# Products of zeros among the first transposes and projections, and one weight load moved ahead of another

## The chip, the cores and the metric

The kernel runs on one core of a Trainium2 chip. The metric is the device time of one execution in microseconds; lower is better. The engines are named as in the profile: PE is TensorE (matrix products, its weight loads shown apart as PEld), DVE is VectorE, ACT is ScalarE, POOL is GpSimd and SP is SyncE, which here only issues DMA transfers.

## The reference

One layer of a hybrid decoder on 1024 tokens of width 1024, with 16 meta tokens put in front, all in float32:

```python
u = rmsnorm(h, g_pre_mix[l])
z = u @ w_in[l]
q, k, v, xr, yr = jnp.split(z, split_at, axis=-1)
attn = sliding_window_attention_with_sinks(...)
...                                  # conv(4), gated linear recurrence, GeLU gate
mix = jnp.concatenate([attn.astype(h.dtype), rec], axis=-1) @ w_out[l]
h = h + rmsnorm(mix, g_post_mix[l])
u = rmsnorm(h, g_pre_ffn[l])
f = jnp.square(jax.nn.relu(u @ w_ff1[l])) @ w_ff2[l]
h = h + rmsnorm(f, g_post_ffn[l])
```

`w_in` is 1024 x 1792, `w_ff1` 1024 x 4096 and `w_ff2` 4096 x 1024.

## The kernel before, in words

Every float32 operand is split into a high and a low part, and a product is made of three products: high by high, high by low, low by high. `mm3` issues the three at lines 125, 130 and 131; `part` (line 309) issues one of the three for all eight blocks `kc` of 128 rows, and `project` uses `mm3`. A split is a cast on ACT (line 96) and a subtraction on DVE (line 99).

The token rows are normalised, transposed on PE, 128 columns at a time, and split into `u`, eight pairs of tiles tagged "a". The tokens come in four pieces; the first one, `ALL[0]`, has 272 rows: 16 meta rows `xm` and two blocks `xa` and `xb` of 128 rows each. `transposed_first` handles it. Its inner function `turn` (line 401) chains the transposes in a fixed order: six blocks of `xa`, the gains `g_r`, six blocks of `xm`, six blocks of `xb`. Blocks `kc` 6 and 7 are transposed whole (line 426), once the banks of blocks 0 and 1 have been read. After each block, `split_scaled` scales and casts it on ACT (line 117) and subtracts on DVE (line 118). The first projections of K and V then follow through `part` (line 309): `wk` high by `u` high, `wk` high by `u` low, the same for `wv`, and the third parts.

PE has nothing to do until the first rows are normalised. In that time `load` (line 339) issues products of a tile of zeros into a bank `idle` that nobody reads: 11 of them, each of 512 columns.

A scheduler that estimates times orders the instructions of each engine at build time; `behind` and `chained` add fixed orders where they are wanted. Tiles come from pools by tag ("raw", "ws", "a", "b", "c", "d", "e"), each with a number of buffers, and a new tile waits until the buffer that it gets is free. The PSUM banks come from four tags of two banks each ("acc", "pt", "o", "s").

Behind the attention, the recurrence and the output projection stands the feed-forward part. Its first product is done by blocks with sums of blocks (a Strassen-like scheme): `prep_a(p)` loads two tiles `r0` and `r1` of `w_ff1` (512 KB each, `w1_load`, line 1185), forms sums of their halves on DVE (line 1188) and splits them. Some blocks are wanted before any sum and are loaded alone by `early`: two loads of 256 KB each. The last call, `early(1, 2, pair("a", ESH), "a")`, fills an "a" tile; `loads[0]` holds the name of its last load. `prep_a` puts the load of `r0` behind that load and leaves the load of `r1` free. All of these loads go through SP's queue, in the order in which the scheduler put them.

Of the kernel before, what the change touches and what calls it, by code (L numbers as in the profile page):

```python
# [10 lines left out]
F32R = mybir.dt.float32r  # L11
# [5 lines left out]
P = 128  # L17
# [20 lines left out]
def hybrid_layer(  # L38
# [6 lines left out]
    nc = tc.nc  # L45
# [12 lines left out]
    def slot(tag, shape, dt=F32):  # L58
        uid[0] += 1
        return slab.tile(shape, dt, tag=tag, name=f"{tag}{uid[0]}", bufs=bufs[tag])  # L60
# [242 lines left out]
            sink(acc[:, :n], t0, n)  # L303


    def part(acc, w, piece, k, last=2):
        t0, n = piece
        for kc in range(KC):
            last_mm[0] = nc.tensor.matmul(  # L309
                acc[:, :n], w[k // 2][:, kc, :], u[kc][k % 2][:, t0 : t0 + n],  # L310
                start=k == 0 and kc == 0, stop=k == last and kc == KC - 1,
                skip_group_check=True,
            ).ins.name

    ALL = [(0, 272), (272, 256), (528, 256), (784, 256)]
    REAL2 = [(16, 512), (528, 512)]
# [7 lines left out]
    for h in range(2):  # L324
        nc.gpsimd.memset(f32(kl[h][HALF[1 - h]]), 0.0)

    zeros = slot("ws", [P, 512], F32R)
    nc.vector.memset(f32(zeros), 0.0)
    km = slot("ws", [P, 4, 2 * P], F32R)
    nc.gpsimd.memset(f32(km[:, 0:2, 0 : P - NMETA]), 0.0)  # L330
# [3 lines left out]


    idle = bank("acc")
    def load(n, cols, after=None):
        for _ in range(n):
            ins = nc.tensor.matmul(
                idle[:, :cols], zeros[:, :P], zeros[:, :cols], start=True, stop=True,  # L340
                skip_group_check=True,
            ).ins
            if after:
                behind(after, ins)
        return ins.name

    load(11, 512)

    def normed(b):
        if b == 0:  # L350
# [12 lines left out]
    def chained(e, ins):  # L363
        if last[e] is not None:
            behind(last[e], ins)
        last[e] = ins.name
# [29 lines left out]
    def transposed_first(xn):  # L396
        (xm, _), (xa, _), (xb, _) = xn
        n, order = ALL[0][1], [None]

        def turn(dst, src):  # L400
            ins = nc.tensor.transpose(dst, src, ident[: src.shape[0], : src.shape[0]]).ins
            if order[0]:
                behind(order[0], ins)
            order[0] = ins.name

        def cols(kc):
            return slice(kc * P, (kc + 1) * P)

        pts = []
        for kc in range(6):  # L410
            pts.append(bank(("o", "s", "pt")[kc % 3]))
            turn(pts[kc][:, NMETA : NMETA + P], xa[:, cols(kc)])
        pg = bank("acc")
        turn(pg[:, :8], g_r)
        chained(0, nc.scalar.copy(g_mix_col, pg[:, :8]).ins)
        for kc in range(6):
            turn(pts[kc][:, :NMETA], xm[:NMETA, cols(kc)])
        for kc in range(KC):
            if kc < 6:
                pt = pts[kc]  # L420
                turn(pt[:, NMETA + P : n], xb[:, cols(kc)])
            else:
                pt = bank(("o", "s")[kc - 6])
                o = 0
                for x_, m in xn:
                    nc.tensor.transpose(pt[:, o : o + m], x_[:m, cols(kc)], ident[:m, :m])
                    o += m
            uh, ul = u[kc]
            high = split_scaled(
                uh[:, :n], ul[:, :n], pt[:, :n], g_mix_col[:, kc : kc + 1]  # L430
            )
            chained(0, high[0])
            chained(1, high[1])
            mark[0] = high[1].name

    def fetch(cols, tag="raw", pieces=1):
        raw = slot(tag, [P, KC, P])
# [25 lines left out]
    chained(0, nc.scalar.copy(wk[0][:, 0:4], rk[:, 0:4]).ins)  # L463
    last[1] = scaled[0]
    chained(1, nc.vector.tensor_copy(wk[0][:, 4:8], rk[:, 4:8]).ins)
    transposed_first(xn)
    low_w(wk, rk)
    wv = high_w(rv, "b")
    low_w(wv, rv)
# [89 lines left out]
    for b in range(4):  # L559
        if b:  # L560
            transposed(b, xn if b == 1 else normed(b), done[b])
        piece = ALL[b]
        if b == 0:

            acc = [bank("acc"), bank("acc")]
            for a, w in zip(acc, (wk, wv)):
                part(a, w, piece, 0)
                part(a, w, piece, 1)
            xn = [(norm_rows(xt[2], True), P)]
            xn.append((norm_rows(xt[3], True), P))  # L570
            part(acc[0], wk, piece, 2)
            sink_k(acc[0][:, : piece[1]], *piece)
            part(acc[1], wv, piece, 2)
            sink_v(acc[1][:, : piece[1]], *piece)
            wq1 = high_w(rq1)
            low_w(wq1, rq1)
            for w, (t0, n), sink, tag in (
                (wq, (16, 256), sink_q0, "o"), (wq1, (16, 256), sink_q1, "acc"),
            ):
                acc = bank(tag)  # L580
                for k in range(3):
                    part(acc, w, (t0, n), k)
# [631 lines left out]
    def prep_a(p, late=None):  # L1214
        r0 = slot("raw", [P, 4, 256])
        behind(loads[0], w1_load(r0, 0, p, 0, 2))
        r1 = slot("a" if 2 <= p < 14 else "d", [P, 4, 256])
        w1_load(r1, 1, p, 0, 2)
        a11, a21, a12, a22 = r0[:, :, LO], r0[:, :, HI], r1[:, :, LO], r1[:, :, HI]
        sums = [  # L1220
            combine(a22, a21, a22, ALU.add), combine(a21, a11, a21, ALU.subtract)
# [514 lines left out]
```

## Time and profile before

| | |
|---|---|
| median of 3 runs | 944.97 us (944.78 to 945.34) |
| the profiled execution's own time | 945.26 us |
| its span, first to last instruction | 943.3 us |
| PE busy | 934.0 us (99%) |
| DVE, ACT, POOL busy | 664.7, 505.1, 132.9 us |
| mean granted TensorE clock | 0.999 |
| PE's first product of zeros starts | 1.51 us |
| the first transpose starts | 6.94 us |
| the first projection product starts | 9.57 us |

Times inside a run are microseconds from the first instruction. In a row of the timeline stand the start, the duration, the engine, the line, the operation, the tiles (output <- inputs), the shape, how many instructions were merged into the row, and in brackets how long the engine had been idle and what ended that. The duration of a PE product holds the way through the array too, so products overlap: how fast they follow one another is seen from their starts.

### The profile page before, as it was taken

To read this page: it belongs to the slowest core of one execution; us is meant where nothing else is said; L and a number is where in the kernel's file an instruction comes from. 1 tells how busy PE (TensorE), PEld (TensorE's weight loads), DVE (VectorE), ACT (ScalarE), POOL (GpSimd) and SP (SyncE) were. 2 spreads that over 40 slices of the span, in tenths; PEclk is the share of its full clock that TensorE was granted. 3 is DMA by queue.
4 is the path that set the end of the run, shared out by engine and by line. 5 is a ranking of instruction groups with operands and counts; after the bars stand their busy time and mean duration, and the time that the engine had idled before them with its cause. 6 is when DMAs were issued, how large, how long until landed. Compare 5 with 4: busy or idle time off the path is not lost.

```text
span 943.3 us, 12158 instructions
## 1 busy us (share of the span) xinstructions
PE 934.0 (99%) x4562; PEld 780.8 (83%) x4562; DVE 664.7 (70%) x846; ACT 505.1 (54%) x846; POOL 132.9 (14%) x204
## 2 busy tenths in 40 slices
PE   8999999999999999999999999999999999999997
PEld 7999999877888888888888888888888888888886
DVE  7667788889877986755544465477667676779794
ACT  8546765679434854443655575653533443445441
POOL 4104436430021200110000000001121000001200
PEclk9999999999999999999999999999999999999999
DMA  8220011104359768573422364334777755647934
GB/s 275 58 67 23 24 46 46 46 23 142 101 182 291 234 192 287 180 255 123 157 89 90 116 219 120 103 113 115 198 171 177 210 179 189 191 155 208 242 65 90
DMA packets 99911, 136.49 MB, mean 145 GB/s; under 512 B 24391, under 2 KB 63319, under 8 KB 99853
## 3 DMA queue, kind: packets, MB, share of 16 engines
q1 hardware_dynamic: 90652, 110.67, 36.7%
q0 software_dynamic: 8736, 23.67, 11.8%
q10 hardware_dynamic: 464, 1.38, 0.4%
q8 instruction: 36, 0.59, 0.3%
q14 instruction: 23, 0.18, 0.1%
HBM read 113.60 MB, written 21.50 MB: 143 GB/s over the span
## 4 chain that ended last, share of the span: by engine, by line
PE 98%; DVE 0%; DMA 0%; ACT 0%; issue 0%; DVEq 0%; ACTq 0%
PE ps_acc L125 12%; PE ps_acc L131 11%; PE ps_acc L130 11%; PE ps_pt L130 7%; PE ps_pt L125 7%; PE ps_pt L131 7%; PE ps_s L125 6%; PE ps_s L131 6%; PE ps_s L130 6%; PE ps_o L125 5%; PE ps_o L130 5%; PE ps_o L131 5%; PE ps_o L763 2%; PE ps_acc L988 1%; PE ps_acc L309 1%; PE ps_s L693 1%
## 5 line engine op out<-in xcount | busy, mean ns | idle before, releaser
L99 DVE TENSOR_TENSOR ws<-raw,ws 128x1024 fp32r<-128x1024 f32 (+1 forms) x69 | 83.6, 1212 | 74.3 <-ACT ws L96 23.3
L96 ACT CAST ws<-raw 128x1024 fp32r<-128x1024 f32 (+1 forms) x68 | 69.7, 1026 | 80.8 <-PE ps_o L130 32.6
L96 ACT CAST ws<-e 128x1024 fp32r<-128x1024 f32 x41 | 43.0, 1050 | 84.9 <-PE ps_o L130 37.8
L99 DVE TENSOR_TENSOR b<-b,b 128x1024 fp32r<-128x1024 f32 (+1 forms) x49 | 57.7, 1179 | 27.0 <-PE ps_o L130 21.7
L130 PE MATMUL ps_acc<-a,ws 128*128 128x512 f32 (+3 forms) x224 | 76.3, 341 | 0.0
L125 PE MATMUL ps_acc<-a,ws 128*128 128x512 f32 (+3 forms) x224 | 76.3, 341 | 0.0
L131 PE MATMUL ps_acc<-a,ws 128*128 128x512 f32 (+3 forms) x224 | 75.7, 338 | 0.0
L99 DVE TENSOR_TENSOR ws<-e,ws 128x1024 fp32r<-128x1024 f32 x41 | 50.2, 1224 | 31.2 <-ACT ws L96 17.8
L96 ACT CAST b<-b 128x1024 fp32r<-128x1024 f32 (+1 forms) x49 | 49.5, 1011 | 41.5 <-DVE b L1188 35.3
L750 POOL TENSOR_SCALAR_AFFINE_SELECT c<-c 128x512 fp32r<-128x512 f32 x64 | 51.4, 817 | 75.2 <-ACT c L96 66.1
L131 PE MATMUL ps_acc<-ws,b 128*128 128x512 f32 (+1 forms) x120 | 46.1, 384 | 0.0
L130 PE MATMUL ps_acc<-ws,b 128*128 128x512 f32 (+1 forms) x120 | 46.1, 384 | 0.0
L125 PE MATMUL ps_acc<-ws,b 128*128 128x512 f32 (+1 forms) x120 | 46.0, 385 | 0.0
L125 PEld LDWEIGHTS ps_acc<-a,ws 128*128 128x128 f32 x224 | 42.2, 188 | 3.1 <-DVE b L997 0.3
L131 PEld LDWEIGHTS ps_acc<-a,ws 128*128 128x128 f32 x224 | 42.2, 188 | 3.0
L130 PEld LDWEIGHTS ps_acc<-a,ws 128*128 128x128 f32 x224 | 42.1, 188 | 2.8
L130 PE MATMUL ps_pt<-ws,b 128*128 128x512 f32 x112 | 44.2, 395 | 0.0
L125 PE MATMUL ps_pt<-ws,b 128*128 128x512 f32 x112 | 44.2, 394 | 0.0
L131 PE MATMUL ps_pt<-ws,b 128*128 128x512 f32 x112 | 44.0, 393 | 0.0
L125 PE MATMUL ps_s<-ws,b 128*128 128x512 f32 x110 | 43.4, 395 | 0.0
L130 PE MATMUL ps_s<-ws,b 128*128 128x512 f32 x110 | 43.3, 393 | 0.0
L131 PE MATMUL ps_s<-ws,b 128*128 128x512 f32 x110 | 43.2, 393 | 0.0
(436 smaller groups left out, 2679.8 us busy)
## 6 DMA issues: line engine op xcount, KB each, us to landing
raw<-in_w_ff_dram SPq DMA_DIRECT2D x59, 512.0 KB
e<-in_w_ff_dram SPq DMA_DIRECT2D x43, 512.0 KB
a<-in_w_ff_dram SPq DMA_DIRECT2D x12, 512.0 KB
s_dram<-a POOLq DMA_DIRECT2D x12, 512.0 KB, 3.8
raw<-in_w_in_dram SPq DMA_DIRECT2D x9, 512.0 KB
c<-in_x_dram SPq DMA_DIRECT2D x8, 512.0 KB
d<-in_x_dram SPq DMA_DIRECT2D x8, 512.0 KB
out_dram<-raw SPq DMA_DIRECT2D x8, 512.0 KB
```

Of the source, the lines that this page charges most:

```text
L96: cast[0] = nc.scalar.copy(hi, src).ins.name
L99: low = nc.vector.tensor_tensor(lo, src, f32(hi), op=ALU.subtract).ins
L125: ins = nc.tensor.matmul(dst, lh, rh, start=start, stop=False, skip_group_check=True).ins
L130: nc.tensor.matmul(dst, lh, rl, start=False, stop=False, skip_group_check=True)
L131: last_mm[0] = nc.tensor.matmul(dst, ll, rh, start=False, stop=stop, skip_group_check=True).ins.name
L309: last_mm[0] = nc.tensor.matmul(acc[:, :n], w[k // 2][:, kc, :], u[kc][k % 2][:, t0 : t0 + n], start=k == 0 and kc == 0, stop=k == last an ...
L693: nc.tensor.matmul(dst, q[h][:, c], hi, start=True, stop=False, skip_group_check=True,)
L750: nc.gpsimd.affine_select(out=p_[:, :, s], in_=f32(p_[:, :, 0]), pattern=[[0, 4], [g, P]], compare_op=op, fill=0.0, base=0, channel_multip ...
L763: nc.tensor.matmul(two[:, :, oc : oc + w], v, p_.rearrange("p (j i) s c -> p j (i s c)", j=2)[:, :, pc : pc + w], start=n == 0 and k == 0, ...
L988: ins = nc.tensor.matmul(y2_bank[half], (wh, wh, wl)[k][:, kc, :], (uh, ul, uh)[k][:, t0 : t0 + n], start=m % 24 == 0, stop=m % 24 == 23, ...
```

## The change

It has four parts.

1. `zeros` has 128 columns where it had 512. The products of 512 columns read it four times over, through an operand that repeats the one block.
2. In front of the first transposes stand 13 products of zeros instead of 11.
3. Ten more products of zeros, of 128 columns each, go into a bank `pad` at fixed places: two in front of the transposes of `xb`, two behind them, and behind the first products of `part` two, one, one, none, none, one and one for `kc` 0 to 6 (`PADS`).
4. `prep_a(0)` puts the load of `r1`, too, behind `early`'s last load.

```diff
-    def part(acc, w, piece, k, last=2):
+    def part(acc, w, piece, k, last=2, pads=None):
         t0, n = piece
         for kc in range(KC):
-            last_mm[0] = nc.tensor.matmul(
+            ins = nc.tensor.matmul(
...
+            if pads and kc < len(pads[0]):
+                behind(pads[2], ins)
+                pads[2] = load(pads[0][kc], pads[1], ins.name)
+            last_mm[0] = ins.name
...
-    zeros = slot("ws", [P, 512], F32R)
+    zeros = slot("ws", [P, P], F32R)
...
-    def load(n, cols, after=None):
+
+    def load(n, dst, after=None):
+        cols = dst.shape[-1]
+        rhs = zeros
+        if cols > P:
+            dst = dst.rearrange("p (a b) -> p a b", b=P)
+            rhs = zeros.rearrange("p (a b) -> p a b", a=1).to_broadcast([P, cols // P, P])
         for _ in range(n):
             ins = nc.tensor.matmul(
-                idle[:, :cols], zeros[:, :P], zeros[:, :cols], start=True, stop=True,
-                skip_group_check=True,
+                dst, zeros, rhs, start=True, stop=True, skip_group_check=True
             ).ins
...
-    load(11, 512)
+    load(13, idle)
...
+        pad = bank("acc")
         for kc in range(6):
             turn(pts[kc][:, :NMETA], xm[:NMETA, cols(kc)])
+        order[0] = load(2, pad[:, :P], order[0])
         for kc in range(KC):
+            if kc == 6:
+                order[0] = load(2, pad[:, :P], order[0])
...
+        return [PADS, pad[:, :P], order[0]]
+
+    PADS = (2, 1, 1, 0, 0, 1, 1)
...
-                part(a, w, piece, 0)
+                part(a, w, piece, 0, pads=pads)
+                pads = None
...
-        w1_load(r1, 1, p, 0, 2)
+        ins = w1_load(r1, 1, p, 0, 2)
+        if p == 0:
+            behind(loads[0], ins)
```

The instruction streams differ at these places and nowhere else, apart from which semaphore a few instructions wait on. The first place is on PE, from the last transpose of `xb` to the first projection products. `ps_acc_262` (later `ps_acc_269`) is the bank of the K projection, `ps_o_223` and `ps_s_229` (`ps_o_230`, `ps_s_236`) are the banks of blocks 6 and 7. Before:

```order
L401 MATMUL ps_pt_194<-ident,d_147 128x128
L309 MATMUL ps_acc_262<-a_89,b_180 128x272
L309 MATMUL ps_acc_262<-a_91,b_180 128x272
L426 MATMUL ps_o_223<-ident,d_128 128x16
L426 MATMUL ps_o_223<-ident,d_135 128x128
L426 MATMUL ps_o_223<-ident,d_147 128x128
L309 MATMUL ps_acc_262<-a_93,b_180 128x272
L426 MATMUL ps_s_229<-ident,d_128 128x16
L426 MATMUL ps_s_229<-ident,d_135 128x128
L426 MATMUL ps_s_229<-ident,d_147 128x128
```

In the changed kernel, at the same place on PE, where line 349 is the product of zeros and `ps_acc_201` the bank `pad` (lines 309, 411 and 440 are 309, 401 and 426 of before):

```order
L411 MATMUL ps_pt_196<-ident,d_149 128x128
L349 MATMUL ps_acc_201<-ws_111 128x128 x2
L309 MATMUL ps_acc_269<-a_89,b_182 128x272
L349 MATMUL ps_acc_201<-ws_111 128x128 x2
L309 MATMUL ps_acc_269<-a_91,b_182 128x272
L349 MATMUL ps_acc_201<-ws_111 128x128
L440 MATMUL ps_o_230<-ident,d_130 128x16
L440 MATMUL ps_o_230<-ident,d_137 128x128
L440 MATMUL ps_o_230<-ident,d_149 128x128
L309 MATMUL ps_acc_269<-a_93,b_182 128x272
L349 MATMUL ps_acc_201<-ws_111 128x128
L440 MATMUL ps_s_236<-ident,d_130 128x16
```

The transposes and projection products keep their order; a product of zeros now stands ahead of each group of whole transposes, too.

The second place is in SP's queue, around the start of the feed-forward part. `d_3559` (later `d_3572`) is `r1` of `prep_a(0)`, `a_3494` (`a_3507`) is the "a" tile of `early`'s last call, `raw_3557` (`raw_3570`) is `r0` of `prep_a(0)`. Before, with the semaphores that each load waits for:

```order
L1129 DMA out_dram<-raw_3333 128x1024 [waits DVE_49]
L1185 DMA d_3559<-in_w_ff_dram 128x4x256 [waits PE_49]
L1185 DMA a_3494<-in_w_ff_dram 128x4x128 [waits DMAHW7_49]
L1185 DMA a_3494<-in_w_ff_dram 128x4x128 [waits DMAHW0_49]
L1185 DMA raw_3557<-in_w_ff_dram 128x4x256 [waits DMAHW5_49,DMAHW1_49,Activation_49]
```

In the changed kernel, in the same place of SP's queue:

```order
L1147 DMA out_dram<-raw_3346 128x1024 [waits DVE_49]
L1203 DMA a_3507<-in_w_ff_dram 128x4x128 [waits PE_49]
L1203 DMA a_3507<-in_w_ff_dram 128x4x128 [waits DMAHW7_49]
L1203 DMA d_3572<-in_w_ff_dram 128x4x256 [waits DMAHW0_49,PE_49]
L1203 DMA raw_3570<-in_w_ff_dram 128x4x256 [waits DMAHW5_49,DMAHW1_49,Activation_49]
```

The 512 KB load of `r1` went behind the two loads of 256 KB; the load of `r0` stays fourth.

More of the change, by code (lines that the diff above doesn't have):

```diff
@@ L312, in part @@
                 skip_group_check=True,
-            ).ins.name
+            ).ins
+            if pads and kc < len(pads[0]):
+                behind(pads[2], ins)
+                pads[2] = load(pads[0][kc], pads[1], ins.name)
+            last_mm[0] = ins.name
     ALL = [(0, 272), (272, 256), (528, 256), (784, 256)]
@@ L344, in load @@
                 behind(after, ins)
-        return ins.name
-    load(11, 512)
+            after = ins.name
+        return after
+    load(13, idle)
     def normed(b):
@@ L465, in hybrid_layer @@
     chained(1, nc.vector.tensor_copy(wk[0][:, 4:8], rk[:, 4:8]).ins)
-    transposed_first(xn)
+    pads = transposed_first(xn)
     low_w(wk, rk)
```

## Prediction

> **What bounds the kernel now.** I read the page first: the span, the busy shares, the granted clock and the chain of waits by engine.
>
> ```profile
> span 943.3 us, 12158 instructions
> PE 934.0 (99%) x4562; PEld 780.8 (83%) x4562; DVE 664.7 (70%) x846; ACT 505.1 (54%) x846; POOL 132.9 (14%) x204
> PEclk9999999999999999999999999999999999999999
> PE 98%; DVE 0%; DMA 0%; ACT 0%; issue 0%; DVEq 0%; ACTq 0%
> ```
>
> PE is busy for 99% of the span, at full granted clock in every slice, and it is 98% of the chain that ended last. A change can save time only where PE waits or where its own products become fewer or faster. So the second view is the list of waits of PE over the whole span, and the third is busy time by windows (columns: the window, its length, then busy us and instruction count of PE, PEld, DVE, ACT and POOL, the granted clock, the DMA share, GB/s).
>
> ```profile
> PE ps_acc L339 <- DVE base_e L627: 1.5, 1, 1.5
> PE ps_o L401 <- DVE d L248: 1.0, 2, 0.8
> ```
>
> ```profile
> 6.20:9.50 3.30, 2.34 (x19) 1.85 (x19) 2.94 (x8) 2.38 (x7) 0.20 (x1) 1.00 1.19 325
> 9.50:12.20 2.70, 2.63 (x13) 1.78 (x13) 2.65 (x7) 2.70 (x9) 0.00 (x0) 1.00 1.12 326
> 12.20:300.00 287.80, 287.74 (x1712) 254.91 (x1712) 230.39 (x353) 176.42 (x412) 85.65 (x134) 1.00 0.30 91
> 300.00:350.00 50.00, 50.00 (x230) 40.67 (x229) 41.70 (x66) 37.21 (x71) 6.77 (x11) 1.00 0.72 224
> 350.00:930.00 580.00, 580.00 (x2537) 472.30 (x2536) 377.84 (x396) 280.56 (x337) 34.72 (x40) 1.00 0.55 162
> ```
>
> The two waits both lie in the first 9 us. From 12.20 to 930 PE is busy for 917.74 of 917.80 us. Two things follow. The load that moves in SP's queue, near 314, has no PE wait to remove. And whatever the first 12 us lose or gain reaches the end in full, because nothing behind them has slack.
>
> The fourth view is the timeline of those 12 us.
>
> ```profile
> 0.98 0.48 DVE L328 MEMSET ws<- 128x512 f32 x1 [0.98 <-PEq L1720]
> 1.41 0.06 DVE L627 MEMSET base_e<- 128x4 f32 x1
> 1.51 4.66 PE L339 MATMUL ps_acc<-ws 128*128 128x512 f32 x11 [1.51 <-DVE base_e L627]
> 6.94 0.30 PE L401 MATMUL ps_o<-ident,d 128*128 128x128 f32 x1 [0.77 <-DVE d L248]
> 7.07 0.27 PE L401 MATMUL ps_s<-ident,d 128*128 128x128 f32 x1
> 7.18 0.27 PE L401 MATMUL ps_pt<-ident,d 128*128 128x128 f32 x1
> ...
> 8.16 0.21 PE L401 MATMUL ps_s<-ident,d 16*128 16x16 f32 x1
> 8.22 0.21 PE L401 MATMUL ps_pt<-ident,d 16*128 16x16 f32 x1
> 8.63 0.30 PE L401 MATMUL ps_o<-ident,d 128*128 128x128 f32 x1 [0.20 <-DVE d L248]
> 9.03 0.49 ACT L117 ACTIVATE a<-ps_o,gcol 128x272 fp32r<-128x272 f32 x1 [0.89 <-PE ps_o L401]
> 9.20 0.27 PE L401 MATMUL ps_pt<-ident,d 128*128 128x128 f32 x1
> 9.55 0.50 DVE L118 SCALAR_TENSOR_TENSOR a<-ps_o,gcol,a 128x272 fp32r<-128x272 f32 x1 [0.34 <-ACT a L117]
> 9.56 0.19 PEld L309 LDWEIGHTS ps_acc<-a,b 128*128 128x128 f32 x1 [0.33 <-ACT a L117]
> 9.94 0.19 PEld L309 LDWEIGHTS ps_acc<-a,b 128*128 128x128 f32 x1 [0.19 <-ACT a L117]
> 10.27 0.60 PE L426 MATMUL ps_o<-ident,d 16*128 16x16 f32 x3
> 10.62 0.37 PE L309 MATMUL ps_acc<-a,b 128*128 128x272 f32 x1
> 10.93 0.60 PE L426 MATMUL ps_s<-ident,d 16*128 16x16 f32 x3
> 11.26 0.52 ACT L117 ACTIVATE a<-ps_o,gcol 128x272 fp32r<-128x272 f32 x1
> 11.28 5.31 PE L309 MATMUL ps_acc<-a,b 128*128 128x272 f32 x37
> 11.63 0.53 ACT L117 ACTIVATE a<-ps_s,gcol 128x272 fp32r<-128x272 f32 x1
> 12.21 4.17 PEld L309 LDWEIGHTS ps_acc<-a,b 128*128 128x128 f32 x33 [0.19 <-ACT a L117]
> ```
>
> PE sits behind others here. The first transpose waits for DVE's normalised rows (0.77 us idle), the transposes of `xb` wait for DVE again (0.20), and the first eight projection products follow ACT, which casts one block after another: 9.03 for the first, 11.26 and 11.63 for the last two, so one each 0.37 us. The last of them lets PE go at 12.21, and from there PE streams.
>
> **The change part by part.** The profiled execution took 945.26 us, its span 943.3 and 1.96 around it; it lies 0.29 above the median of the runs, 944.97. The sum below is made against the execution and then moved to the median.
>
> *Smaller tile of zeros.* Filling 512 columns took 0.48 us and 4 columns 0.06, so 128 columns are estimated, on the line between, at 0.16. The products of zeros start 0.32 earlier, at 1.19. DVE idles behind the fill until its rows arrive, so nothing else moves. Worth nothing by itself.
>
> *Two more products in front.* The speed of such a product changes on the way:
>
> ```profile
> L339 PE MATMUL ps_acc<-ws x11: 397/628/796, 1.5 to 5.8; 128*128 128x512 f32 x11
> 317.70 0.39 PE L125 MATMUL ps_s<-b,b 128*128 128x512 f32 x1
> 317.93 0.39 PE L130 MATMUL ps_s<-b,b 128*128 128x512 f32 x1
> ```
>
> The eleven start between 1.5 and 5.8, so they follow each other by 0.43 at the median duration of 628 ns; a product of this size later follows by 0.23 (317.70 to 317.93). The shortest, 397 ns, has the duration of those later ones, so the speed doubled near the end of the eleven; I put it at 5.5, some 4.0 us behind the first. The granted-clock column does not show the slow start; the durations do. Two more cost 0.46 to 0.86. The eleven ended at 6.17, so the thirteen end between 6.17 - 0.32 + 0.46 = 6.31 and 6.71. The first transpose waits for DVE until 6.94, which covers them. If all thirteen ran slowly, they would end at 1.19 + 0.80 + 12 x 0.43 = 7.15, 0.21 late. I take 0, bounds 0 and +0.21.
>
> *Ten small products.* No row has a product of this type with 128 columns. The nearest are the transposes of 128 columns, which follow each other by 0.11 (7.07 to 7.18); I take 0.11 for each. [...]
>
> I stay with the row, for each of the ten:
>
> - Two ahead of the transposes of `xb`: small transposes follow each other by 0.06 (8.16 to 8.22), so PE is free near 8.28, and 0.22 more end at 8.50. DVE lets the next go at 8.63. Hidden; at twice the price 0.09 late.
> - Two behind those: 9.20 + 0.11 + 0.22 = 9.53, and ACT lets the first projection product go at 9.56. Hidden, by little, but a delay here does not reach ACT, whose input is ready.
> - Two behind the first projection product: a product of 272 columns takes 0.14 at most (5.31 for 37), so 9.56 + 0.14 + 0.22 = 9.92, before the next at 9.94. Hidden.
> - One behind the second: 9.94 + 0.14 + 0.11 = 10.19. The transposes of block 6 start at 10.27, since their bank is read by DVE until 9.55 + 0.50 = 10.05. Hidden, or up to 0.11 late if the time from 10.05 to 10.27 is PE's own.
> - One behind the third, at 10.62. The transposes of block 7 followed at 10.93 with no wait that the profile shows, and ended at 10.93 + 0.60 = 11.53. Between the end of a first transpose (8.63 + 0.30 = 8.93) and ACT's cast (9.03) lie 0.10, and 11.53 + 0.10 is 11.63: ACT's last cast has no slack. This product costs 0.11, through ACT and the last projection product, to the end; 0 if it fits into the 0.17 between 10.62 + 0.14 and 10.93.
> - The two behind the sixth and seventh run while PE waits for ACT (0.19 idle ahead of 12.21). Hidden.
>
> Sum: +0.11; lower bound 0, since nothing that sets 6.94, 8.63 or ACT's pace gets faster; upper bound with the thirteen late as well, 0.21 + 0.09 + 0.11 + 0.11 = +0.52.
>
> *The load moved in SP's queue.* Today `r1` ("d") is issued first, then the two halves of the "a" tile.
>
> ```profile
> 313.64 0.43 SPq L1185 DMA_DIRECT2D d<-in_w_ff_dram  x1
> 314.12 1.58 SPq L1185 DMA_DIRECT2D a<-in_w_ff_dram  x2
> 320.11 1.05 ACT L96 CAST a<-a 128x1024 fp32r<-128x1024 f32 x1 [0.63 <-DMA a<-in_w_ff_dram]
> 322.39 0.69 DVE L1188 TENSOR_TENSOR d<-raw,d 128x512 f32<-128x512 f32 x1
> 330.56 0.39 PE L125 MATMUL ps_pt<-b,a 128*128 128x512 f32 x1
> ```
>
> Afterwards the "a" halves go first. The 1 MB of the three lands by 320.11, whatever its order. `r1` then comes last, at about 320.1, and DVE wants it at 322.39: 2.3 us of slack. The "a" tile is cast up to 0.63 earlier, but PE takes it only at 330.56. The new wait of the "a" load on PE cannot hold the queue: before, it stood behind `r1`, whose own wait on PE covered it. I take 0; below nothing is excluded because PE has no wait there, and above nothing takes more than 2.3 us of delay.
>
> So the profiled execution would become 945.26 + 0.11 = 945.37, and the median 944.97 + 0.11 = 945.08.
>
> **The rivals.**
>
> *The clock falls back today, and the small products prevent it (faster).* Between the end of the zeros at 6.17 and the first projection product at 9.57, PE has 3.4 us with only transposes and waits. If PE then lost its speed and took 4.0 us to regain it, as at the start, it would run slowly until 13.6. From 12.21 that is 1.4 us at half speed, 0.7 lost. A median that holds such executions would fall to 944.97 - 0.7 = 944.3. For it speaks how long the stretch is. Against it: in this execution the clock column is 1.00 in both windows, the products from 11.28 on take 0.14 each, and three runs lie within 0.56 us. [...]
>
> *The repeated operand runs slower (slower).* No row shows a product that reads one block four times. The thirteen have 6.94 - 1.19 = 5.75 us, 0.44 each; from there on they delay the first transpose. Were each the price of four transposes, 0.44 fast and 0.88 slow, about 4.6 would run in the 4.0 slow us and 8.4 x 0.44 = 3.7 follow: they end at 8.9, 1.95 late. The slack ahead of 8.63 (8.28 to 8.63) takes back 0.35, so 1.6 stay: 946.6. If the speed never doubled, 13 x 0.88 ends at 12.6, 5.7 late and 5.3 net: 950.3. Against it: four pieces of one operand are still 512 columns in one instruction.
>
> *`r1` lands late (slower).* Behind two other loads it could come later than 322.39; DVE is busy 41.70 of 50 us in that window and would push its splits back, and PE would wait for the excess over 2.3 us. It would take a landing of 4.2 us later than I expect to be seen: 946.9.
>
> *The change does nothing*: all products hide, 944.97. That is my lower bound; it lies in the forecast.
>
> **How the numbers follow.** The measurement can tell about 0.2%, 1.9 us, from no change. The forecast, 0 to +0.5, has 0.80; the clock rival 0.10, of which 0.03 for more than one fall and so over 1.9 us; the repeated operand 0.06, of which 0.05 over 1.9 us; the late `r1` 0.02, half of it visible; other causes 0.02, half to each side. Faster: 0.03 + 0.01 = 0.04. Slower: 0.05 + 0.01 + 0.01 = 0.07. Within: 0.89. The runs scatter from 944.78 to 945.34; with 0 to +0.5 that is 944.78 to 945.86. Downwards the range takes in the clock rival at 944.3, with 0.1 below it, and upwards 0.14 for another scatter of the runs: 944.2 to 946.0.
>
> **What would show it right or wrong.** Right: the products of zeros end before 6.94; the first transpose, 8.63 and 9.03 stay; block 7's transposes and ACT's last cast come about 0.1 later; the last projection weight load stands near 12.3; PE still shows no wait from there to 930; the "a" cast near 319.5 and `r1`'s sum still at 322.4. Wrong: a first transpose behind 6.94 that waits for PE itself (repeated operand); products of 272 columns at 0.23 or more (clock); a wait of PE between 322 and 345 (`r1`); or a shift at 12.21 that does not reappear at the end.

## The result, and the profile after

The changed kernel takes 946.86 us (median of 20 runs, 945.12 to 947.57), the kernel before took 945.08 in the same comparison (20 runs, 944.71 to 946.62): a ratio of 1.0014, with an interval of 1.0008 to 1.0020. The prediction was 945.1, with a range of 944.2 to 946.0. (The ratio of the two medians is 1.0019, that of the means 1.0014.) Single runs scatter by over 2 us, with 16 of the changed kernel's 20 and 2 of before's 20 above 946, so a profile need not be typical: the changed kernel's took 945.68 (span 943.6) and is one of its shortest runs, the one of before took 945.26.

The first 12 us of the changed kernel, in the timeline:

```profile
0.90 0.17 DVE L332 MEMSET ws<- 128x128 f32 x1 [0.90 <-PEq L1740]
1.12 4.81 PE L349 MATMUL ps_acc<-ws 128*128 128x512 f32 x13 [1.12 <-DVE base_e L645]
6.96 0.30 PE L411 MATMUL ps_o<-ident,d 128*128 128x128 f32 x1 [1.03 <-DVE d L248]
8.66 0.30 PE L411 MATMUL ps_o<-ident,d 128*128 128x128 f32 x1
9.06 0.49 ACT L117 ACTIVATE a<-ps_o,gcol 128x272 fp32r<-128x272 f32 x1 [0.89 <-PE ps_o L411]
9.83 0.33 PE L349 MATMUL ps_acc<-ws 128*128 128x128 f32 x2
10.20 0.22 PE L349 MATMUL ps_acc<-ws 128*128 128x128 f32 x1
11.08 0.60 PE L440 MATMUL ps_s<-ident,d 16*128 16x16 f32 x3
11.71 0.49 ACT L117 ACTIVATE a<-ps_s,gcol 128x272 fp32r<-128x272 f32 x1
12.25 0.42 PEld L309 LDWEIGHTS ps_acc<-a,b 128*128 128x128 f32 x3
```

The thirteen products end at 1.12 + 4.81 = 5.93 and PE then waits 1.03 for DVE, as before. Block 7's transposes come at 11.08 for 10.93, ACT's last cast at 11.71 for 11.63, the last wait for ACT ends at 12.25 for 12.21. That is the +0.1 of the sum, at 0.04 to 0.08.

The rest of the loss lies over 300 us further on. SP's queue, the sum of `prep_a(0)` on DVE, and the products of PE near 333, from the timelines of the changed kernel:

```profile
313.60 1.32 SPq L1203 DMA_DIRECT2D a<-in_w_ff_dram  x2
315.02 0.64 SPq L1203 DMA_DIRECT2D d<-in_w_ff_dram  x1
317.95 0.37 SPq L1203 DMA_DIRECT2D raw<-in_w_ff_dram  x1
319.34 1.05 ACT L96 CAST a<-a 128x1024 fp32r<-128x1024 f32 x1
323.87 0.69 DVE L1206 TENSOR_TENSOR d<-raw,d 128x512 f32<-128x512 f32 x1 [1.44 <-DMA raw<-in_w_ff_dram]
324.48 0.75 DVE L1161 TENSOR_SCALAR d<-raw,rs 128x1024 f32<-128x1024 f32 x1
333.14 1.69 ACT L96 CAST b<-a 128x256 fp32r<-128x256 f32 x3 [0.22 <-DVE a L1206]
333.17 0.40 PE L131 MATMUL ps_pt<-b,a 128*128 128x512 f32 x1
333.58 0.76 DVE L99 TENSOR_TENSOR b<-a,b 128x256 fp32r<-128x256 f32 x2
333.60 0.50 PE L125 MATMUL ps_acc<-b,e 128*128 128x512 f32 x1
334.06 0.50 PE L130 MATMUL ps_acc<-b,e 128*128 128x512 f32 x1
334.40 0.39 PE L131 MATMUL ps_acc<-b,e 128*128 128x512 f32 x1
```

The same places in the kernel before:

```profile
323.84 0.75 DVE L1143 TENSOR_SCALAR d<-raw,rs 128x1024 f32<-128x1024 f32 x1 [0.77 <-POOL rs L172]
332.52 1.70 ACT L96 CAST b<-a 128x256 fp32r<-128x256 f32 x3 [0.22 <-DVE a L1188]
332.95 0.77 DVE L99 TENSOR_TENSOR b<-a,b 128x256 fp32r<-128x256 f32 x2
333.13 0.39 PE L131 MATMUL ps_pt<-b,a 128*128 128x512 f32 x1
333.36 0.40 PE L125 MATMUL ps_acc<-b,e 128*128 128x512 f32 x1
333.59 0.40 PE L130 MATMUL ps_acc<-b,e 128*128 128x512 f32 x1
```

DVE's sum started at 322.39 before and starts at 323.87 now, behind a wait of 1.44 us for the `raw` tile, which is `r0`. The scale behind it comes at 324.48 for 323.84, 0.64 later. The last splits of `t_sums`, whose results PE reads as `b`, come as much later nine microseconds on: ACT's casts at 333.14 for 332.52, DVE's lows at 333.58 for 332.95. Nothing is made up on the way. In before, PE took the first cast at 333.36, 0.84 behind its start; here it takes it at 333.60, 0.46 behind, so before had 0.38 us in hand, and 0.62 less 0.38 is lost at once: the product comes 0.24 later. (The products ahead of it ran 0.04 later, at 333.17 for 333.13.) Then PE meets the later casts and lows. Its products follow by 0.43, 0.46 and 0.34 us, where 0.23 each is their pace in before (333.13, 333.36, 333.59): 0.54 us lost. The busy time of PE in the window 300:350 (columns as in the prediction) hides most of that, since a waiting product is shown longer (the one at 333.60 as 0.50, for 0.40 at 333.36 in before):

```profile
300.00:350.00 50.00, 49.97 (x227) 40.20 (x226) 41.10 (x65) 36.84 (x70) 6.37 (x11) 1.00 0.72 221
```

PE does 227 products in it where it did 230.

### The profile page after: what moved, and what is told of

Read it like the earlier page. It is cut to its first block, busy times and chain, and to the rows that moved or that the text cites. A ratio compares the mean times of both kernels' runs of the same rounds, so it can differ in the third digit from the quotient of the medians.

```text
span 943.6 us, 12181 instructions
## 1 busy us (share of the span) xinstructions
PE 935.0 (99%) x4574; PEld 781.9 (83%) x4574; DVE 664.5 (70%) x846; ACT 505.2 (54%) x846; POOL 134.4 (14%) x204
## 4 chain that ended last, share of the span: by engine, by line
PE 99%; DMA 0%; DVE 0%; ACT 0%; DVEq 0%; issue 0%
PE ps_acc L125 12%; PE ps_acc L130 11%; PE ps_acc L131 11%; PE ps_pt L130 7%; PE ps_pt L125 7%; PE ps_pt L131 7%; PE ps_s L125 6%; PE ps_s L131 6%; PE ps_s L130 6%; PE ps_o L125 5%; PE ps_o L130 5%; PE ps_o L131 5%; PE ps_o L781 2%; PE ps_acc L1006 1%; PE ps_acc L309 1%; PE ps_s L711 1%
```

## The experiments

Theory S: the whole loss is the moved load; `r0` lands later, DVE waits for it, and PE for DVE. The rivals are named with each run. In each comparison the kernel before ran on the same chip. It had medians of 945.19, 945.04, 944.87 and 945.06 in the four, and lay above 946 in 19 of its 128 runs, those of the result included.

**The change once more.** No edit.

> The changed kernel once more, for a second profile of it. Theory A (SP's queue): r1 stands behind the two halves of the a tile, the loads around it land late, the sums of prep_a(0) wait on DVE and PE waits near 333; the excess over before in the median (1.8 us) is that wait, so this profile shows PE gaps between 333 and 345 of 0.5 to 2.5 us in total, as much as its own time is above 945.1. Theory B (zeros): the excess comes from the first 14 us, the last projection weight load of the first eight stands between 12.3 and 14, and the gaps near 333 stay at 0.6 or less whatever the time.

Measured 947.02 (946.12 to 947.43, 11 runs, all above 946), ratio 1.0016 [1.0007, 1.0025]. The profiled run, 946.57, is longer than the first one, and shows the same place with a larger wait:

```profile
324.72 0.69 DVE L1206 TENSOR_TENSOR d<-raw,d 128x512 f32<-128x512 f32 x1 [1.65 <-DMA raw<-in_w_ff_dram]
334.45 0.49 PE L125 MATMUL ps_acc<-b,e 128*128 128x512 f32 x1 [0.69 <-ACT b L96]
```

**The load alone.** The kernel before, with part 4.

```diff
-        w1_load(r1, 1, p, 0, 2)
+        ins = w1_load(r1, 1, p, 0, 2)
+        if p == 0:
+            behind(loads[0], ins)
```

> The kernel before with part 4 alone: the load of r1 of prep_a(0) behind early's last load, no change to the products of zeros. Theory A: +1.3 to +1.9 us over before, DVE's first sum of prep_a(0) waits for its loads by 1 to 4 us and PE has gaps near 333. Theory B: within 0.3 us of before.

Measured 947.03 (945.16 to 947.57, 9 of 11 runs above 946), ratio 1.0013 [1.0004, 1.0021]. DVE waits 2.61 us, PE 1.23, and PE's busy time in the window 330:350 is that much short:

```profile
325.07 0.69 DVE L1188 TENSOR_TENSOR d<-raw,d 128x512 f32<-128x512 f32 x1 [2.61 <-DMA raw<-in_w_ff_dram]
334.80 0.50 PE L125 MATMUL ps_acc<-b,e 128*128 128x512 f32 x1 [1.23 <-ACT b L96]
330.00:350.00 20.00, 18.77 (x80) 14.47 (x79) 16.80 (x31) 12.90 (x21) 1.73 (x3) 1.00 0.61 196
```

**The zeros alone, and the front alone.** The changed kernel without part 4, and the kernel before with parts 1 and 2.

```diff
# zeros alone
-        ins = w1_load(r1, 1, p, 0, 2)
-        if p == 0:
-            behind(loads[0], ins)
+        w1_load(r1, 1, p, 0, 2)
# front alone: parts 1 and 2, no small products
-    load(11, 512)
+    load(13, idle)
```

> The changed kernel without part 4: the small tile of zeros, 13 products in front and the ten small ones, and SP's queue as before. Theory A: +0.05 to +0.3 us over before (the 0.11 of the prediction), no PE gap near 333. Theory B: +1.3 to +1.9 us.

> The kernel before with parts 1 and 2 alone: the tile of zeros of 128 columns and 13 products in front, none of the ten small ones. Theory A: within 0.2 us of before. Theory B, if the repeated operand or the clock is at fault: more than +1 us; if the ten small products are at fault: within 0.2 us of before while the run without part 4 shows the excess.

Measured 945.02 (3 of 11 runs above 946), ratio 0.9999 [0.9990, 1.0008], and 945.18 (1 of 11), ratio 0.9997 [0.9988, 1.0006]. The products of zeros are worth nothing that can be measured; the loss is part 4. The profile of the zeros alone happens to be one of its three long runs, 946.68, with the same signature, a sum at 324.93 behind `r0`. Its load order is that of before, so the weak place is there without part 4, and is met less often.

Half of the long runs of before, and the longest of them, have another mark, though. For 108 of its runs, those of the four comparisons, the mean granted clock is on record. 17 of them lie above 946 us, and 9 of these 17 have a clock of 0.994 to 0.997, where most of its runs have 0.998 or 0.999. Of the nine above 946.5, eight have the lower clock. Over all kernels, `shift` (below) left aside, 19 of 171 runs without the ten small products have it, and none of 99 runs with them. No run of before with the lower clock was kept as a trace, so where the clock fell in it is not shown.

**When `r0` lands.** The traces of before and of the changed kernel hold 16 semaphore events for `r0`, from 321.25 to 321.71 and from 321.10 to 323.75; they are counted here as portions of the load that have landed. From these events, in us, with the order in SP's queue:

```
kernel       order in the queue   r0 issued   14 of 16   last     sum starts
before       r1, a, a, r0         317.99      321.61     321.71   322.39
front alone  r1, a, a, r0         318.22      321.91     322.12   322.62
zeros alone  r1, a, a, r0         318.59      322.71     324.85   324.93
after        a, a, r1, r0         317.95      321.86     323.75   323.87
after again  a, a, r1, r0         318.06      322.96     324.60   324.72
load alone   a, a, r1, r0         317.94      322.15     324.95   325.07
```

The bulk of `r0`, 14 portions, lands by 321.6 to 323.0 whatever the order; one or two portions come later, the last of them 1.6 to 2.8 us behind it, in the three traces with `r1` right ahead of `r0` and in the long run of the zeros. DVE waits for the last portion: the sum starts 0.12 us behind it in the three traces of part 4, at 323.87 for 323.75, 324.72 for 324.60 and 325.07 for 324.95.

**More time for DVE.** The sums that read `r0` behind the last combine of `t_sums(8:12)`, in the changed kernel and in the kernel before.

```diff
-    t_sums(slice(8, 12))
-    wa[0] = prep_a(0)
+    summed_8 = t_sums(slice(8, 12))
+    wa[0] = prep_a(0, summed_8)
```

> The changed kernel, with prep_a(0)'s two sums put behind the last combine of t_sums(8:12), so that DVE does four sums, a scale and one low, some 3 us of work, before it first needs r0. Theory S (the whole loss is DVE waiting at its sum for r0's last portions, and the lows of ot2 coming late to PE behind that): no idle time of PE near 333, even if r0 still lands at 323.5 to 325, and a median of 945.0 +- 0.4, with few runs above 946. Theory P (part 4 costs PE something by itself, by its waits or its traffic, wherever DVE stands): still about 946.9, most runs above 946. If the reordering itself costs (r1, r0's splits come later to the first products that read them), PE waits at another place, between 334 and 345, and the time is above 946 with that gap in the trace.

> The kernel before, with the same reordering on DVE and nothing else. Theory S: before has the same exposure, with its r0 landing at 321.7 for a want at 322.39, so that about one run in five is at 947; with the reordering these go, the median is 944.9 to 945.1 and no more than one run in ten lies above 946. If the runs of before at 947 have another cause than r0, the share above 946 stays near one in five.

Both missed: 947.81 (ratio 1.0028 [1.0017, 1.0039]) and 947.34 (1.0026 [1.0016, 1.0036]). `r0`, landed at 324.86 and 321.92, no longer holds DVE, but DVE now has nothing to do while it waits for the scale's input and for ACT. From the kernel before with this edit, and a wait of PE in the changed kernel with it:

```profile
323.24 0.75 DVE L1143 TENSOR_SCALAR d<-raw,rs 128x1024 f32<-128x1024 f32 x1 [0.76 <-POOL rs L172]
324.73 0.43 DVE L1188 TENSOR_TENSOR a<-c,c 128x256 f32<-128x256 f32 x1 [0.74 <-ACT c L1174]
333.94 0.69 DVE L1308 TENSOR_TENSOR b<-ps_pt,b 128x512 f32<-128x512 f32 x1
334.54 1.89 DVE L99 TENSOR_TENSOR b<-a,b 128x256 fp32r<-128x256 f32 x3
```

```profile
356.15 0.50 PE L131 MATMUL ps_s<-b,e 128*128 128x512 f32 x1 [1.24 <-DVE e L99]
```

The lows stand at 334.54, 1.59 later than in before: the two pauses, and an add of `p2` (L1308) that the scheduler now puts ahead of them. The sums had been moved out of that stretch. PE loses 1.5 us at these lows in both kernels, and more near 353 to 356, where it waits for another split of DVE (last row above): 0.8 in before with the edit, 1.5 in the changed kernel with it. The edit changed the order on DVE and ACT in many places, so it does not test theory S cleanly.

**Another order, and a shift of the instruction stream.** `r1` behind `r0`; and, in the second kernel, 7 products of 512 columns with 50 of 16 columns in place of the 13. The trace of before shows 36 packets of 16,384 bytes of instructions, 13 to 33 us apart, 28 at the median, and in the six traces above one such packet starts between 319.6 and 323.2 and takes 0.93 to 2.29 us.

```diff
# swap
-        behind(loads[0], w1_load(r0, 0, p, 0, 2))
+        first = w1_load(r0, 0, p, 0, 2)
+        behind(loads[0], first)
...
-            behind(loads[0], ins)
+            behind(first.name, ins)
# shift
-    load(13, idle)
+    load(7, idle)
+    for _ in range(50):
+        nc.tensor.matmul(idle[:16, :16], zeros[:, :16], zeros[:, :16], ...)
```

> The changed kernel with r1 behind r0 in SP's queue: the two halves of the a tile, r0, r1. Theory Q (r1's 512 KB, in flight when r0 is issued near 318, delay r0): r0 lands by about 321.5, r1 becomes the last and lands at 322.5 to 324; DVE's first sum reads both, so it still waits and the time stays near 947. Theory R (it is the place near 320 to 324 that is slow, whatever is loaded): the same. What tells them apart is r0's own landing: before 321.9 by Q, 323 or later in R. If the time falls to 945.0 and the sum does not wait, then r1 ahead of r0 was the cost and a queue that issues r0 first mends it.

> The changed kernel, with 7 products of zeros of 512 columns and 50 of 16 columns in front instead of the 13, so that PE's stream of instructions is 44 longer and the fetches of instructions fall some 10 us earlier in relation to the loads. Theory M (a 16 KB packet of instructions near 320 holds up one DMA engine and with it one portion of r0): the packet leaves the window 318 to 324, r0's last portion lands by 322 and the runs are in one group, at 945.0 plus whatever the start loses (0 to 2 us: read from the first projection product), without a gap of PE near 333. If the packet is not the cause: r0's last portion still lands at 323.5 or later, with PE's gap near 333 of 0.6 us or more, and most runs lie 1 to 2 us above the fastest.

`swap` took 946.83, ratio 1.0017 [1.0008, 1.0026]. `r0` came earlier, 15 portions by 321.64 and the last at 323.19, but `r1` landed at 324.61 and the sum, which reads both, waited for that (2.23 us). The last portion, at 323.19, is what R said, the other 15 are what Q said: the run does not decide between them. `shift` took 949.13, 1.0039 [1.0027, 1.0052]; its profiled run, 948.39, lost most of it at the start (last section). Its packet of instructions fell at 312.5, before the loads, and still three portions of `r0` straggled: issued at 320.28, 13 landed by 324.34, the last at 326.48, and DVE waited 1.39. So the packet is not the cause, or not the only one. Where one portion alone came late (`r0` in the zeros alone, both loads in `swap`), a packet did run while `r0` was landing, from 320.25 to 322.55 and from 320.88 to 322.10; that it held that portion up is not shown.

**`r1` in two loads of 512-byte packets.** The order on PE, ACT and DVE near the place stays.

```diff
         r0 = slot("raw", [P, 4, 256])
+        r1 = slot("a" if 2 <= p < 14 else "d", [P, 4, 256])
+        if p == 0:
+            for k in range(2):
+                ins = w1_load(r1[:, :, k * P : k * P + P], 1, p, k, k + 1)
+                behind(loads[0], ins)
+                loads[0] = ins.name
         behind(loads[0], w1_load(r0, 0, p, 0, 2))
...
```

> The changed kernel with r1's 512 KB loaded by two loads of 256 KB with packets of 512 B, at the same place in SP's queue (behind the two halves of the a tile, ahead of r0); nothing else moves on any engine. Theory E (engines that fall behind in r1's load of 1,024-B packets, 14 of 16 portions by 319.64 and two by 320.44, are served r0 last; where loads of 512-B packets stand between, as in before, the lag stays what it was): the portions of r0 land within 0.7 us of each other, by 322.2, and the median is 945.0 to 945.3. Theory F (what counts is that 256 KB more stand ahead of r0 in the last stretch, whatever the packets): r0's last portion still lands at 323.5 to 325, and the median is 946.5 to 947.

Between the two theories: 946.20 (945.15 to 947.73, 6 of 11 above 946), ratio 1.0010 [1.0001, 1.0019]. `r1`'s second half landed within 0.64 us, yet three portions of `r0` came at 323.20 to 323.92. What makes portions straggle stays open.

**Less pause for DVE.** The sums behind the scale alone, in the changed kernel and in before; then the same with the add of `p2(2)` held behind the lows.

```diff
-    wa[0] = prep_a(0)
+    wa[0] = prep_a(0, scaled_7[0])
# held, too
-    p2(2, a12_early[2])
+    p2(2, a12_early[2], lows=urgent)
```

> The changed kernel, with prep_a(0)'s two sums put behind DVE's scale of the last block (L1161) instead of behind the last combine of t_sums. In the kernel with the sums put far back, DVE idled twice for 0.76 and 0.78 us at 322.4 to 324.7, before the scale and before t_sums, and had nothing to fill them with; here the scale stands at about 323.2 and the sum at 323.9, between the two. Theory S (DVE works without a pause from the scale to 344, so each idle 0.1 us there reaches PE near 333): r0 is needed at 323.9 instead of 322.39, 1.5 us of the lateness are free, DVE's work ends where it does in before, and the median is 945.0 to 945.4, with PE's gap near 333 at or under 0.3 us unless r0 lands behind 324.3. Theory P (part 4 costs PE by something else than the wait of the sum): 946.9 again.

> The kernel before, with the same reordering of the sums alone. Theory S: r0 lands at 321.7 to 322.1, needed at 323.9; no PE gap near 333, median 944.9 to 945.1, and none of the runs near 947, if those runs of before come from r0. If the share near 947 stays at one in five, they have another cause. If DVE's reordering costs by itself, a PE gap between 330 and 345 shows it, and the median goes above 945.5.

> The changed kernel, with the two sums of prep_a(0) behind the scale (as in after_scale) and p2(2)'s add held behind the lows of t_sums(12:16), where it stood in the changed kernel. Theory S: what after_scale lost, it lost to that add (0.6 us ahead of the lows); without it the lows start by 333.2 to 333.6 unless r0 lands behind 324.3, and the median is 945.0 to 945.6. Theory P: 946.5 or more, as in after_scale.

> The kernel before, with the sums behind the scale and p2(2)'s add held behind the lows. Theory S: 945.0, with PE gaps near 333 of under 0.2 us; before_scale's 946.57 was the add, not the sums. If it stays above 946, putting the sums behind the scale costs by itself.

Measured 946.48 (ratio 1.0015 [1.0007, 1.0024]) and 946.57 (1.0019 [1.0010, 1.0028]) without the hold, 946.92 (1.0013 [1.0005, 1.0022]) and 945.56 (1.0006 [0.9997, 1.0015]) with it. On the kernel before, the hold took 946.57 to 945.56, so the add was most of what `before_scale` lost. Not all of it: in the trace of `before_hold` the scale still comes first, held to 323.82 by a pause of 0.78, the sum follows at 324.49, and PE loses 0.90 at 333, so the order itself costs. The changed kernel stayed at 946.9 against the 945.0 to 945.6 expected. In its profiled run PE loses 1.59 there, 0.69 more than in `before_hold`, and `r0` landed at 324.87, beyond the 324.3 that the expectation set as its limit:

```profile
322.98 0.75 DVE L1161 TENSOR_SCALAR d<-raw,rs 128x1024 f32<-128x1024 f32 x1 [0.76 <-POOL rs L172]
325.00 0.69 DVE L1208 TENSOR_TENSOR d<-raw,d 128x512 f32<-128x512 f32 x1 [1.26 <-DMA raw<-in_w_ff_dram]
334.46 0.50 PE L125 MATMUL ps_acc<-b,e 128*128 128x512 f32 x1 [1.10 <-ACT b L96]
```

**The lows earlier.** One add of 0.6 us (L1374, in before L1354) behind the lows instead of ahead of them.

```diff
-    nc.vector.tensor_tensor(block("11", 1), y2, block("11", 1), op=ALU.add)
     t_sums(slice(12, 16))
     urgent = mark[0]
+    behind(urgent, combine(block("11", 1), y2, block("11", 1), ALU.add))
```

> The changed kernel, with DVE's add of the second half-product of block 1 (L1374, 0.6 us) put behind the two lows of t_sums(12:16) that PE takes near 333, instead of ahead of their sums. Theory S (what PE waits for near 333 is the lows, and the lows are late by DVE's wait for r0): the lows come 0.6 us earlier in DVE's queue, so that a lateness of 0.7 us at the sum leaves a PE gap of 0 to 0.2 us and one of 1.3 us leaves 0.4 to 0.7; the median falls from 946.9 to 945.0 to 945.9. Theory P (part 4 costs PE elsewhere): 946.9 stays.

> The kernel before, with the same add behind the lows. Theory S: median as before, 945.0, and fewer than one run in ten above 946, since a late r0 now has 0.8 us instead of 0.2 us before PE feels it. If the add's reader or its bank is the next to wait, PE shows a gap behind 336 and the time is above 945.5.

Missed: 948.14 (ratio 1.0032 [1.0020, 1.0044]) and 946.56 (1.0010 [1.0001, 1.0019]). The waits of PE in the kernel before with this edit, and the row of the third:

```profile
PE ps_acc L339 <- DVE base_e L627: 1.5, 1, 1.5
PE ps_o L401 <- DVE d L248: 1.3, 2, 1.1
PE ps_s L125 <- ACT e L96: 1.2, 1, 1.2
343.44 0.50 PE L125 MATMUL ps_s<-b,e 128*128 128x512 f32 x1 [1.19 <-ACT e L96]
```

The gap at 333 is gone: the lows come at 332.60. But PE now waits 1.19 us at 343.44 for the next operand. The edit had also put the splits of the next blocks, on ACT and DVE, into another order, and the cast that PE waits for there is one of them: which part of the edit made that wait is not separated. The changed kernel with the edit has both waits, 0.34 at 333.70 and 1.21 at 344.52.

**Does the account close?** In seven of these traces DVE, ACT and PE do the same work in the same order around 333 as in before, so each product of PE can be set against the same product there. How late the sum of `prep_a(0)` starts, against 322.39, is counted less what PE is already late by near 316; what PE loses at 333 is how much later it is near 335 than near 316. In us:

```
              sum later   PE later   sum's own   PE loses
                          at 316     lateness    at 333     difference
after           1.48        0.05       1.43        0.55        0.88
split           1.65        0.09       1.56        0.68        0.88
after again     2.33        0.25       2.08        1.19        0.89
swap            2.34        0.04       2.30        1.39        0.91
zeros alone     2.54        0.28       2.26        1.38        0.88
load alone      2.68        0.07       2.61        1.72        0.89
shift           4.22        2.47       1.75        0.86        0.89
```

So PE loses the sum's own lateness less 0.9 us, with and without the products of zeros and whatever the order in the queue. The 0.9 can be read from the changed kernel's profile beside that of before: the pause ahead of the scale takes up 0.84 (the sum comes 1.48 later, the scale 0.64), PE's margin takes up 0.38, and 0.33 is lost again at the next two products. In `front alone` the sum's own lateness is -0.05, and PE loses 0.01.

How much later than in before PE is, for all traces, and the time of the profiled run (a name with `after_` is an edit of the changed kernel, one with `before_` the same edit of the kernel before: `slack` the sums far back, `scale` the sums behind the scale, `hold` the add held as well, `lows` the lows earlier):

```
               at 316   lost      lost         last product   time over
                        at 333    behind 335   later          945.26
front alone     0.28     0.01       0.35         0.64          0.25
after           0.05     0.55       0.03         0.62          0.42
split           0.09     0.68       0.03         0.80          0.56
before_hold     0.04     0.90       0.03         0.97          0.58
before_lows    -0.09     0.01       1.57         1.49          0.95
after again     0.25     1.19       0.08         1.51          1.31
swap            0.04     1.39       0.07         1.50          1.31
after_hold     -0.15     1.59       0.11         1.54          1.33
zeros alone     0.28     1.38       0.17         1.82          1.42
after_scale     0.24     1.29       0.37         1.89          1.44
load alone      0.07     1.72       0.03         1.83          1.61
before_slack    0.06     1.49       0.79         2.34          2.13
after_lows     -0.16     0.85       1.87         2.56          2.16
before_scale    0.24     1.17       0.19         1.60          2.21
after_slack     0.04     1.49       1.51         3.03          2.55
shift           2.47     0.86       0.01         3.34          3.13
```

Behind its last product the profile of before takes 0.30 us longer than the others. With that, the last two columns agree within 0.25 us, but for `before_scale`, whose end is 0.8 longer than theirs. Where part 4 is added or removed alone, PE loses next to nothing elsewhere: a second path from the queue to PE isn't needed. What the runs do not show is a kernel with part 4 that returns to 945: each edit that was to give DVE room moved other work, and lost by that.

## Why the prediction was wrong

- **The zeros: right in what they cost.** They end at 5.93, ahead of the 6.94 that mattered and even of the 6.31 to 6.71 given. The prediction let the speed double at 5.5; in this trace the products start 0.43 us apart from 1.71 up to 4.27, and 0.23 to 0.24 apart from 4.61 on. The two small products of the row at 9.83 start 0.06 us apart, those of the pairs at 8.38 and 9.26 0.17 and 0.14, where the prediction took 0.11 for each. The one product that was to cost 0.11 cost 0.04 to 0.08 (12.25 for 12.21, 11.71 for 11.63). Alone, the zeros measured 0.9999.
- **The load moved in SP's queue: the step that failed.** It was taken at 0, with "2.3 us of slack". That slack was `r1`'s, and `r1` kept it: it landed at 320.44 where 320.1 was said, and the "a" cast came at 319.34 where 319.5 was said. But the sum at 322.39 reads `r0` as well, and `r0` landed at 321.71 in before. The slack of the later of its two inputs was 0.68 us, and `r0` is the load issued right behind the one that was moved. The step counted the 1 MB of the three loads and left out the fourth, whose place in the queue stays the same. Its last portions landed 2.0 to 3.2 us later (323.75, 324.60, 324.95), and that cost PE 0.55, 1.19 and 1.72 us. Why they land later is open.
- **The rival "`r1` lands late": the right path, the wrong load.** DVE's splits pushed back and a wait of PE "between 322 and 345" are what happened, and a landing near 324.3 was priced at 1.9 us, where landings of 324.60 and 324.95 cost PE 1.19 and 1.72. But its chance of 0.02 was set by how far `r1` would have to slip, 4.2 us behind what was expected. For `r0` about 1.8 us is enough, as the same two profiles show: the sum starts 0.12 behind the last portion, so `r0` could come by 322.27 without delaying it, and the 0.84 at the scale and the 0.38 at PE put the limit near 323.5. Between the scale and the lows DVE has no pause to make anything up: 0.64 late at the one, 0.63 at the other.
- **"From 12.20 PE streams, so the load has no PE wait to remove": true, and the wrong question.** PE at 100% of the window showed no wait, and had 0.38 us in hand.
- **The repeated operand: rightly dismissed.** The thirteen products follow each other by 0.43 us until the speed doubles, as those of before do, and the front alone moved nothing (0.9997).
- **The clock rival: not in the medians, but there.** It said that the clock falls back in some executions of before and that the small products prevent it. That the stretch of 3.4 us brings such a fall on was the author's supposition: no run varied the stretch alone. The windows from 6.20 to 12.20 show a granted clock of 1.00 in both profiles. But 14 of 108 runs of before have a lower mean clock, and none of 99 with the small products and the thirteen. `front alone`, with the thirteen and without the small ones, has one such run in 11, so which part helps is not settled. The rival's price was for the median, and runs as rare as these hardly move that: the zeros alone are at 0.9999.

## What to carry to other kernels

Where a load is moved in a queue, list every input of the operation that reads it, and the loads issued next to it, with the landing of each; the slack is that of the last one. Where an engine runs without a pause from that operation to the one that the bound engine needs, any delay beyond the pauses and margins on the way arrives whole (here the sum's lateness less 0.9 us), so these must be added up to the far end. And where single runs scatter, traces of several of them, set against one another product by product, show whether one place accounts for all of it; here seven traces lie on one line. Runs can be long for different reasons (here 9 of the 17 long runs of before with a clock on record had 0.994 to 0.997): look at the granted clock of each before putting them down to one.

## What was not expected of the hardware

**In `shift` the clock fell behind the front.** In its profiled run, with 7 products of 512 columns and 50 of 16, the windows show the granted clock (sixth value behind the window's length) at half from 8.80 on, and back by 16:

```profile
6.20:8.80 2.60, 2.16 (x19) 1.95 (x20) 2.56 (x7) 1.68 (x6) 0.20 (x1) 1.00 1.16 331
8.80:12.20 3.40, 3.40 (x18) 3.06 (x17) 2.66 (x8) 2.80 (x7) 0.00 (x0) 0.50 1.14 341
12.20:14.50 2.30, 2.30 (x11) 2.30 (x12) 1.63 (x3) 1.66 (x3) 0.00 (x0) 0.50 1.15 315
14.50:16.00 1.50, 1.50 (x10) 1.50 (x9) 1.50 (x2) 1.50 (x2) 0.00 (x0) 0.61 1.04 342
16.00:20.00 4.00, 4.00 (x35) 4.00 (x34) 2.47 (x4) 2.25 (x7) 2.92 (x4) 1.00 0.98 365
```

The first projection product, from the timelines of `shift` and of the changed kernel:

```profile
9.51 0.54 PE L309 MATMUL ps_acc<-a,b 128*128 128x272 f32 x1
```

```profile
9.60 0.39 PE L309 MATMUL ps_acc<-a,b 128*128 128x272 f32 x1
```

It takes 0.54 us for 0.39, and the loads at 314 were issued 2.8 us later (316.38 for 313.60). Products of 16 columns from 4.27 to 5.79, a wait of 0.85 us and transposes from 6.64 on stood in front of the fall; which of them brought it about is not separated. Of the other four runs one has a mean clock of 0.997 (947.75 us); the three longest, 949.13 to 949.58, have 0.999, so they show no fall of this size, and what slowed them is not shown.

**DVE pauses ahead of the scale in nine of the 17 traces.** In the kernel before, in `before_slack` and in `after_hold` the scale starts 0.76 to 0.77 us behind the end of DVE's operation ahead of it (rows above: 323.84, 323.24 and 322.98), released by POOL's `rs`; four more traces have 0.76 to 0.78. In `front alone` and in `before_lows` the pause is 0.46. In the other eight, where DVE had stood idle for a load just ahead of it (1.44 us in the changed kernel), there is none. POOL's rows in before and the scale in `front alone`:

```profile
322.29 0.86 POOL L166 TENSOR_SCALAR ms<-ssq 128x1 f32<-128x1 f32 x1 [4.74 <-ACT d L1131]
323.24 0.57 POOL L172 TENSOR_TENSOR rs<-ms,half_pow 128x1 f32<-128x1 f32 x1
```

```profile
323.76 0.75 DVE L1157 TENSOR_SCALAR d<-raw,rs 128x1024 f32<-128x1024 f32 x1 [0.46 <-POOL rs L172]
```

The step at L166 takes 0.86 here and ends at 323.15, just behind DVE's sum (322.39 to 323.08); in `front alone` it takes 0.22, from 322.58 on, with DVE busy too, and the step at L172 behind it takes 0.84 for 0.57 in before. What makes the one step or the other longer is not shown: no run varied it alone. In `before_slack` the pause moved with the scale: the scale came 0.60 earlier, and the sums were still to be done.
